# Softmax attention: values in two parts held still in TensorE, weights divided before they are turned, outputs by feature

## The chip, the core and the metric

One core of a Trainium2 chip runs the whole program in one launch. The metric is device time in microseconds (us): 2874.34 us is the median of 3 runs (2862.95 to 2874.93). The engines named below: TensorE (PE; its weight load is PEld), VectorE (DVE), ScalarE (ACT), GpSimd (POOL), and SyncE (SP), which issues nearly all transfers. TensorE writes to PSUM (8 banks of 128 x 512 fp32); the other tiles lie in SBUF, 128 partitions wide.

## The reference

Two small networks run one behind the other on 512 tokens of width 1024: two layers of mixer, cross attention and MLP, then two layers of mixer and mixture of experts. The change bears on the softmax attentions over 512 tokens with 64 features a head:

```python
# forgetting: 8 heads; causal
p = softmax(where(mask, q @ k.T * scale + c_q - c_k, -inf)); out = p @ v
# dilated: 8 heads, three dilation patterns merged; sliding window of 128 with a sink: 8 heads
out = num * w / (den * w + exp(sink - m2))
# nsa: 16 heads in 4 groups; three branches, gated and added
o_cmp = masked_softmax(q @ kc.T + bias) @ vc         # 31 compressed keys
o_sel = masked_softmax(q @ k_sel.T + bias) @ v_sel   # causal
o_win = masked_softmax(q @ k_win.T + bias) @ v_win   # causal
return gt[0] * o_cmp + gt[1] * o_sel + gt[2] * o_win
```

Everything is float32. With 512 tokens the selection and the window of nsa take in every causal key, so these two branches are plain causal attention.

## The kernel before

**Exact products from split operands.** A float32 operand is split into a high part in the type `float32r` and the rest: ScalarE copies (`L107`, for weights `L130`), VectorE subtracts (`L108`, `L131`). A linear layer is three `float32r` products (`mm3`, L151 to L153), whose outputs are copied or added from the two banks of tag `lin`. Weights come in pieces of 128 x 1024 (`piece`, L123): buffers `ws` (4), `wh` and `wl` (3 each).

**Attention.** Queries come in four blocks of 128, keys in blocks of 128 up to the query's; 10 pairs of blocks a causal head, 7 for the sliding window. For each head and query block `probs` (L289) makes scores in a PSUM bank of tag `s` (two products, L296; with negated queries, so that the largest weight has the smallest number), VectorE adds the bias strip and takes the minimum (L301, L302: one instruction and a second that reads the accumulator), and ScalarE writes `P`, the exponential, and its sum `den` (L304). `pv` (L307) then turns `P` block by block on TensorE (L312), copies it to SBUF on ScalarE or VectorE in turn (`copy`, L783 on VectorE), and multiplies: the turned weights are the stationary operand and 64 columns of plain fp32 values move past them (L316). All eight outputs of a pair of heads stand in one PSUM bank by query. Only then are they divided (`o_norm`, L318; for nsa `gated`, L1740, with the gates: L1749, L1751), turned to features (`pair_out`, L326, L332) and split for the output layer.

Pairs of heads follow each other: four in `ab` (forgetting), four dilated and four sliding in `cd`, eight in `nsa`, each with two causal branches for two heads and a compressed branch. The projection of the next pair stands between them in the code.

**What sets the order.** The program is written against a tile framework. A tile has a tag, and a tag has so many buffers (`BUFS`, L17; `BANKS` for PSUM); who needs a buffer waits for its last reader. The framework also puts the instructions of each engine in an order of its own, so that projections and output layers stand between those of attention; on the chip each engine goes through its list in that order.

Of the kernel before, what the change touches and what calls it, by code (L numbers as in the profile page):

```python
# [33 lines left out]
class Kern:  # L34
# [235 lines left out]
    def k_parts(self, y, name="K", tag="x"):  # L270
# [3 lines left out]
        K, L = self.pair(name, tag, F32R), self.pair("KL", tag, F32R)  # L274
# [14 lines left out]
    def probs(self, qk, nk, strip, mn, den, extra=None, floor=None):  # L289
# [14 lines left out]
        nc.scalar.activation(P[:, :nk], p[:, :nk], AF.Exp, bias=mn, scale=-1.0, accum_out=den)  # L304
# [13 lines left out]
    def o_norm(self, o, den, heads):  # L318
        r = self.small((128, heads), "rden")
        self.nc.vector.reciprocal(r, den)  # L320
        ob = self.t("ob")
        v = lambda x: x.rearrange("p (h d) -> p h d", h=heads)
        self.nc.vector.tensor_tensor(v(ob), v(o), r[:, :, None].to_broadcast([128, heads, S // heads]), op=OP.mult)
        return ob

# [38 lines left out]
    def ab(self):  # L364
# [8 lines left out]
        v = self.tiles("v", 4, "x")  # L373
# [5 lines left out]
        def ev_v(c, t, p):  # L379
            nc.scalar.activation(v[t][:, c * 256:(c + 1) * 256], p, AF.Copy, scale=rms()[0][:, t:t + 1])  # L380
# [47 lines left out]
        def attend(i):  # L428
            mn, den = self.small((128, 8), "mn"), self.small((128, 8), "den")
            o = self.psum("pt")  # L430
            for j in range(8):
                qb, e = NT - 1 - j // 2, j % 2
                h, nk, qs = 2 * i + e, (qb + 1) * 128, slice(qb * 128, (qb + 1) * 128)
                u = 8 * qb + h
                P = self.probs(self.qk(*parts[i], e, qs, slice(0, nk)), nk, self.fstrip, mn[:, j:j + 1], den[:, j:j + 1],
                               extra=(at[:, u:u + 1].to_broadcast([128, 128]), crh[:, :nk]))
                self.pv(o[:, j * 64:(j + 1) * 64], P, nk, [v[b][:, h * 64:(h + 1) * 64] for b in range(qb + 1)])
            ys[4 + i] = self.pair("y", "y", F32R)
            self.pair_out(self.o_norm(o, den, 8), ys[4 + i])
# [3 lines left out]
        for i in range(4):  # L443
# [6 lines left out]
            attend(i)  # L450
        ys[:4] = [self.rpair("y") for _ in range(4)]
# [71 lines left out]
    def cd(self):  # L523
        nc, V = self.nc, VCOL
        xs, rms = self.rms_prep(self.hT, V["cd_norm"])
        C, Sn = self.pair("CS")
# [12 lines left out]
        v = self.tiles("v", 4, "x")  # L539
        vd_ = self.t("vd")  # L540
        vd = [vd_[:, t * 128:(t + 1) * 128] for t in range(NT)]

        def ev_v(c, t, p):
            nc.scalar.activation(v[t][:, c * 256:(c + 1) * 256] if c < 2 else vd[t], p, AF.Copy, scale=rms()[0][:, t:t + 1])
# [18 lines left out]
        def dilated(i):  # L563
            mn, den = self.small((128, 8), "mn"), self.small((128, 8), "den")
            o = self.psum("pt")
            for j in range(8):
                qb, e = NT - 1 - j // 2, j % 2
                h, nk, qs = 2 * i + e, (qb + 1) * 128, slice(qb * 128, (qb + 1) * 128)
                P = self.probs(self.qk(qp[i], *kp[i], e, qs, slice(0, nk)), nk, self.dstrip[:, 512 - nk:],
                               mn[:, j:j + 1], den[:, j:j + 1])  # L570
                self.pv(o[:, j * 64:(j + 1) * 64], P, nk, [v[b][:, h * 64:(h + 1) * 64] for b in range(qb + 1)])
            self.pair_out(self.o_norm(o, den, 8), ys[i])

        def sliding(i):

            mn, den = self.small((128, 8), "mn"), self.small((128, 8), "den")
            o = self.psum("pt")
            for j in range(8):
                qb, e = NT - 1 - j // 2, j % 2
                h, k0, qs = i + 4 * e, max(0, qb - 1) * 128, slice(qb * 128, (qb + 1) * 128)  # L580
                nk = (qb + 1) * 128 - k0
                P = self.probs(self.qk(qp[4 + i], *kp[4], e, qs, slice(k0, k0 + nk)), nk, self.sstrip[:, 256 - nk:],
                               mn[:, j:j + 1], den[:, j:j + 1], floor=self.nsink[:, h:h + 1])
                self.pv(o[:, j * 64:(j + 1) * 64], P, nk,
                        [vd[k0 // 128 + b][:, e * 64:e * 64 + 64] for b in range(nk // 128)])
            x = self.small((128, 8), "es")
            sinks = self.nsink.rearrange("p (e i) -> p i e", e=2)[:, i]
            nc.vector.tensor_tensor(x.rearrange("p (t e) -> p t e", e=2), mn.rearrange("p (t e) -> p t e", e=2),
                                    sinks[:, None].to_broadcast([128, NT, 2]), op=OP.subtract)
            nc.scalar.activation(x, x, AF.Exp)  # L590
            nc.vector.tensor_tensor(den, den, x, op=OP.add)
            ys.append(self.rpair("y"))
            self.pair_out(self.o_norm(o, den, 8), ys[4 + i])
# [11 lines left out]
        for i in range(8):  # L605
# [5 lines left out]
            (dilated if i < 4 else sliding)(i % 4)  # L611
        for j in range(8):
# [511 lines left out]
    def out_moe(self, wname, ys, layer, out=None):  # L1124

        nc = self.nc
        z = [self.T("z", "y" if layer == 0 else "h") for _ in range(NT)]
# [94 lines left out]
    def ln_out(self, z, layer, out, yg, w, y, ohT, w15):  # L1222
# [16 lines left out]
        def add(t):  # L1239
# [4 lines left out]
            Rs[t] = self.T("R", "h" if layer == 0 else "y")  # L1244
# [63 lines left out]
    def moe(self, layer, lg, Rs, z, rescale):  # L1308
# [76 lines left out]
        xT, oh = self.dispatch(layer, 0, Rs, pos3, iota, "h" if layer == 0 else "y")  # L1385
# [627 lines left out]
```

## Time and profile before

| What | Value |
|---|---|
| Profiled execution | 2872.59 us, of which 2870.8 us are the span of the core |
| TensorE busy | 2684.3 us (94%), weight loads 2290.8 us (80%) |
| VectorE busy | 1783.8 us (62%) |
| ScalarE busy | 1368.9 us (48%) |
| GpSimd busy | 231.1 us (8%) |
| Granted TensorE clock, mean | 0.972 |

Busy shares are means over stages with different limits; the attention stages are some 476 us of the span. A busy TensorE is not one at its peak, since the records of one matmul overlap the next. The same holds on VectorE and ScalarE: a record begins before the one ahead of it has ended.

### The profile page before, as it was taken

How to read it: one execution, taken by the hardware profiler on the slowest of the kernel's cores; microseconds unless marked ns; L12 is line 12 of the kernel's file. 1: busy time of each engine (PE TensorE's matmuls, PEld its weight loads, DVE VectorE, ACT ScalarE, POOL GpSimd, SP SyncE). 2: the span in 40 equal slices, each digit the busy share in tenths (PEclk: the TensorE clock that was granted, in tenths of full speed). 3: DMA queues.
4: the chain of work that ended last, by engine and by line, in shares of the span. 5: the costliest groups of instructions: out<-in, count | busy, mean ns of one | idle time of the engine just before them, and what ended most of it. 6: DMA issues, size and time to landing. Idle time of an engine off the chain costs nothing. (4 is left out here: it accounts for less than half of the span.)

```text
span 2870.8 us, 40089 instructions
## 1 busy us (share of the span) xinstructions
PE 2684.3 (94%) x15088; PEld 2290.8 (80%) x15088; DVE 1783.8 (62%) x3539; ACT 1368.9 (48%) x2545; POOL 231.1 (8%) x207
## 2 busy tenths in 40 slices
PE   8999999999999999999999999969986999986994
PEld 6888888888888988888887888967865888885873
DVE  6675564444457556545347777677766477677667
ACT  5654442333356434332246444327763355525774
POOL 1101010000111010000010000020001011011001
PEclk9999999999999999999999999979998999997998
DMA  4314133333233322335323222327885202013786
GB/s 134 98 56 137 60 107 96 96 95 99 86 88 85 125 78 63 104 100 176 99 93 120 69 69 80 103 65 244 263 282 181 66 23 74 16 49 128 260 264 218
DMA packets 123112, 333.65 MB, mean 116 GB/s; under 512 B 21781, under 2 KB 37813, under 8 KB 122905
## 3 DMA queue, kind: packets, MB, share of 16 engines
q1 hardware_dynamic: 120472, 322.48, 35.8%
q0 software_dynamic: 2432, 8.46, 0.8%
q8 instruction: 124, 2.03, 0.3%
q14 instruction: 84, 0.68, 0.1%
HBM read 301.49 MB, written 29.07 MB: 115 GB/s over the span
## 5 line engine op out<-in xcount | busy, mean ns | idle before, releaser
L130 ACT ACTIVATE wh<-ws 128x1024 fp32r<-128x1024 f32 (+2 forms) x521 | 534.1, 1030 | 888.5 <-PE lin L152 609.5
L131 DVE TENSOR_TENSOR wl<-ws,wh 128x1024 fp32r<-128x1024 f32 (+2 forms) x521 | 622.1, 1199 | 230.8 <-ACT wh L130 228.7
L151 PE MATMUL lin<-xs,wh 128*128 128x512 f32 (+2 forms) x1080 | 427.3, 396 | 7.7 <-ACT xs L196 6.3
L152 PE MATMUL lin<-xs,wh 128*128 128x512 f32 (+2 forms) x1080 | 427.7, 396 | 2.6 <-DVE xs L197 2.6
L153 PE MATMUL lin<-xs,wl 128*128 128x512 f32 (+2 forms) x1080 | 426.5, 395 | 0.9 <-DVE wl L131 0.9
L151 PEld LDWEIGHTS lin<-xs,wh 128*128 128x128 f32 (+2 forms) x1080 | 202.1, 187 | 51.0 <-ACT xs L196 7.2
L152 PEld LDWEIGHTS lin<-xs,wh 128*128 128x128 f32 (+2 forms) x1080 | 202.2, 187 | 47.2 <-DVE xs L197 6.9
L153 PEld LDWEIGHTS lin<-xs,wl 128*128 128x128 f32 (+2 forms) x1080 | 202.1, 187 | 42.1 <-DVE wl L131 1.4
L346 DVE TENSOR_TENSOR h<-lin,h 128x512 f32<-128x512 f32 x112 | 77.4, 691 | 247.7 <-PE lin L153 247.6
L151 PE MATMUL lin<-sr,wh 128*128 128x512 f32 x512 | 199.2, 389 | 0.0
L152 PE MATMUL lin<-sr,wh 128*128 128x512 f32 x512 | 199.2, 389 | 0.0
L153 PE MATMUL lin<-sr,wl 128*128 128x512 f32 x512 | 199.2, 389 | 0.0
L733 DVE SCALAR_TENSOR_TENSOR ra<-lin,bc 128x512 f32<-128x512 f32 x64 | 44.3, 692 | 166.8 <-PE lin L153 164.3
L1519 PE MATMUL o<-oh,Rh 128*128 128x256 f32 x512 | 133.5, 293 | 8.1 <-PEq L1380 4.9
L304 ACT ACTIVATE P<-s,mn 128x256 f32<-128x256 f32 (+1 forms) x224 | 114.2, 514 | 52.4 <-DVE mn L302 50.0
L1519 PE MATMUL o<-oh,Rl 128*128 128x256 f32 x512 | 132.1, 290 | 3.7 <-PEq L1380 3.7
L152 PE MATMUL s<-wl,exh 128*128 128x512 f32 x256 | 106.2, 415 | 12.7 <-DVE wl L131 12.6
L151 PE MATMUL s<-wh,exh 128*128 128x512 f32 x256 | 102.9, 405 | 12.3 <-ACT wh L130 12.1
L153 PEld LDWEIGHTS lin<-sr,wl 128*128 128x128 f32 x512 | 96.1, 188 | 20.1
L152 PEld LDWEIGHTS lin<-sr,wh 128*128 128x128 f32 x512 | 96.1, 188 | 19.9
L151 PEld LDWEIGHTS lin<-sr,wh 128*128 128x128 f32 x512 | 96.1, 188 | 19.8
L1519 PEld LDWEIGHTS o<-oh,Rh 128*128 128x128 f32 x512 | 101.3, 198 | 12.1 <-DVE oh L1508 7.0
(605 smaller groups left out, 6225.0 us busy)
## 6 DMA issues: line engine op xcount, KB each, us to landing
ws<-in_moe_wgu SPq DMA_DIRECT2D x128, 512.0 KB, 5.3
ws<-in_mlp_wu SPq DMA_DIRECT2D x64, 512.0 KB, 3.6
ws<-in_mlp_wd SPq DMA_DIRECT2D x64, 512.0 KB, 3.6
ws<-in_moe_wd SPq DMA_DIRECT2D x64, 512.0 KB, 5.2
yd<-ey SPq DMA_DIRECT2D x60, 256.0 KB, 3.3
ws<-in_gdn_w SPq DMA_DIRECT2D x24, 512.0 KB, 3.6
ws<-in_ab_w SPq DMA_DIRECT2D x16, 512.0 KB, 4.3
ws<-in_xa_wk SPq DMA_DIRECT2D x16, 512.0 KB, 3.8
```

Of the source, the lines that this page charges most:

```text
L130: nc.scalar.activation(wh, ws, AF.Copy)
L131: nc.vector.tensor_tensor(wl, ws, rd(wh), op=OP.subtract)
L151: mm(out, a[0], b[0], start=start, stop=False)
L152: mm(out, a[0], b[1], start=False, stop=False)
L153: mm(out, a[1], b[0], start=False, stop=stop)
L304: nc.scalar.activation(P[:, :nk], p[:, :nk], AF.Exp, bias=mn, scale=-1.0, accum_out=den)
L346: self.nc.vector.tensor_tensor(self.hT[n], p, self.hT[n], op=OP.add)
L733: nc.vector.scalar_tensor_tensor(a, p, 0.0, rms()[1], op0=OP.max, op1=OP.mult)
L1519: nc.tensor.matmul(p[:, j * 256:(j + 1) * 256], Rs[t][i][:, f * 128:(f + 1) * 128], oh[:, t], start=t + i == 0, stop=t == NT - 1 and i == 1)
```

## The change

The values are split too, and both parts of one head, 64 columns high and 64 low, are now the stationary operand. The turned weights move past them, split in two as well, 128 columns a query block, and two query blocks share one instruction. The output stands by feature, high parts in partitions 0 to 63 and low parts in 64 to 127, and `head_out` adds the halves. Since the query now lies along the free axis, the division by `den` (and the gate) moves ahead of the turn: one reciprocal on VectorE and one multiplication on GpSimd for each `P`. `o_norm`, `gated` and `pair_out` go out of these attentions. The sink enters as one more column of the exponential (a small ScalarE copy).

```diff
+        if sink is not None:
+            n += 1
+            nc.scalar.activation(p[:, nk:n], sink, AF.Copy)
+        nc.scalar.activation(P[:, :n], p[:, :n], AF.Exp, bias=mn, scale=-1.0, accum_out=den)
         return P
 
...
+    def weigh(self, P, nk, den, gate=None):
+
+        r = self.small((128, 1), "rd")
+        self.nc.vector.reciprocal(r, den)
+        if gate is None:
+            self.nc.gpsimd.tensor_scalar(P[:, :nk], P[:, :nk], r, None, op0=OP.mult)
+        else:
+            self.nc.gpsimd.tensor_scalar(P[:, :nk], P[:, :nk], r, gate, op0=OP.mult, op1=OP.mult)
+
+    def turn(self, Ps, PT):
+
+        p, n = self.psum("o"), 0
+        for P, nb in Ps:
+            for b in range(nb):
+                self.nc.tensor.transpose(p[:, n * 128:(n + 1) * 128], P[:, b * 128:(b + 1) * 128], self.ident)
...
+        self.split(p[:, :n * 128], *(x[:, :n * 128] for x in PT))
...
+    def causal(self, o, P, V, first=True, last=True):
+
+
+        mm = self.nc.tensor.matmul
+        PT = self.turned()
+        for qb in (3, 2):
+            self.turn([(P(qb), qb + 1)], [x[:, (qb - 2) * 512:(qb - 1) * 512] for x in PT])
+
+        for k, i in ((0, 0), (1, 0), (1, 1), (3, 0), (3, 1), (2, 0), (2, 1), (0, 1)):
+            x = PT[i].rearrange("p (q c) -> p q c", q=2)[:, k // 3:, k * 128:(k + 1) * 128]
+            mm(o[:, 256 + k // 3 * 128:], V(k), x, start=first and k + i == 0, stop=False)
+        PT = [self.t("PT", F32R, "PT") for _ in range(2)]
+        p1 = P(1)
+        self.turn([(P(0), 1), (p1, 2)], PT)
+        for k, i in ((0, 0), (1, 0), (1, 1), (0, 1)):
+            mm(o[:, k * 128:256], V(k), PT[i][:, k * 256:256 + k * 128], start=False, stop=last and (k, i) == (0, 1))
+
+    def head_out(self, e, o, y):
+
+        u = self.t("oh")[:64]
+        self.nc.scalar.activation(u, o[64:], AF.Copy)
+        self.nc.vector.tensor_tensor(y[e * 64:e * 64 + 64], o[:64], u, op=OP.add)
+
+    def v_parts(self, V, p, h, n, r):
+
+        V = V.rearrange("p (h two d) -> p h two d", two=2, d=64)[:, h:h + n]
+        p = p.rearrange("p (h d) -> p h d", d=64)
+        self.nc.scalar.activation(V[:, :, 0], p, AF.Copy, scale=r)
+        self.nc.vector.scalar_tensor_tensor(V[:, :, 1], p, r, rd(V[:, :, 0]), op0=OP.mult, op1=OP.subtract)
 
```

In `ab` (in `cd` likewise; `sliding` makes two turns of two query blocks each, and eight products):

```diff
         def attend(i):
-            mn, den = self.small((128, 8), "mn"), self.small((128, 8), "den")
-            o = self.psum("pt")
-            for j in range(8):
-                qb, e = NT - 1 - j // 2, j % 2
-                h, nk, qs = 2 * i + e, (qb + 1) * 128, slice(qb * 128, (qb + 1) * 128)
-                u = 8 * qb + h
-                P = self.probs(self.qk(*parts[i], e, qs, slice(0, nk)), nk, self.fstrip, mn[:, j:j + 1], den[:, j:j + 1],
-                               extra=(at[:, u:u + 1].to_broadcast([128, 128]), crh[:, :nk]))
-                self.pv(o[:, j * 64:(j + 1) * 64], P, nk, [v[b][:, h * 64:(h + 1) * 64] for b in range(qb + 1)])
+            y = self.t("ob")
+            for e in range(2):
+                h, o = 2 * i + e, self.psum(("pt", "lin")[e])
+
+                def P(qb):
+                    nk, u = (qb + 1) * 128, 8 * qb + h
+                    mn, den = self.small((128, 1), "mn"), self.small((128, 1), "den")
+                    x = self.probs(self.qk(*parts[i], e, slice(nk - 128, nk), slice(0, nk)), nk, self.fstrip, mn, den,
+                                   extra=(at[:, u:u + 1].to_broadcast([128, 128]), crh[:, :nk]))
+                    self.weigh(x, nk, den)
+                    return x
```

In `nsa` the compressed branch is weighted, split and turned at once, and all three branches add up in one PSUM bank a head:

```diff
+            def P(qb):
+                nk, f = (qb + 1) * 128, h * 3 + br + 1
+                mn, den = self.small((128, 1), "mn"), self.small((128, 1), "den")
+                x = self.probs(self.qk(qp[c], *K[c // 4][br], e, slice(nk - 128, nk), slice(0, nk)), nk,
+                               strips[c][:, e * 256 + max(0, 256 - nk):(e + 1) * 256], mn, den)
+                self.weigh(x, nk, den, gt[:, NT - 1 - qb, f:f + 1])
+                return x
+
...
-            L, r = compressed(c)
-            branch(c, 0, acc)
-            if c < 7:
-                if c == 3:
-                    proj_k(1)
-                proj_q(c + 1)
-            compressed_out(c, L, r, acc)
-            branch(c, 1, acc)
```

The wider values need space: they take the four buffers `h`, where the residual stands, during the attentions of `ab` and `cd`. The residual is read again from DRAM after the last head of `ab` (eight transfers of 256 KB, L518 of the new program), and in `cd` written to DRAM at the start (L597) and read back after the dilated heads (L701). In `nsa` the bias strips are loaded pair by pair, and some tiles of the second mixture of experts change places between `h` and `y`.

The new order of each engine. On VectorE, in the middle of `nsa`, before: `L302` are bias and minimum, `PT<-o` is the copy of turned weights, `rg` the reciprocal for a whole pair of heads.

```order
L302 ISA mn_21488 128x1
L783 COPY PT_21558<-o_21554 128x384
L302 ISA s_21589,mn_21488<-s_21589,strip_18300 128x128
L302 ISA mn_21488 128x1
L783 COPY PT_21585<-o_21582 128x256
L302 ISA s_21600,mn_21488<-s_21600,strip_18301 128x128
L302 ISA mn_21488 128x1
L301 TENSOR_REDUCE mf_21671<-s_21667 128x1
L1719 RECIPROCAL rg_21611<-den_21489 128x8
L302 ISA s_21667,mn_21664<-s_21667,strip_18300,mf_21671 128x256
L302 ISA mn_21664 128x1
```

And the same place of the program now: `rd` is the reciprocal of one `P`, `PTwl` and `PT` the low parts of turned weights.

```order
L302 ISA s_24139,mn_24137<-s_24139,strip_23473,mf_24143 128x256
L302 ISA mn_24137 128x1
L335 RECIPROCAL rd_24147<-den_24138 128x1
L301 TENSOR_REDUCE mf_24163<-s_24159 128x1
L108 TENSOR_TENSOR PT_24102<-o_24125,PT_24101 128x384
L302 ISA s_24159,mn_24157<-s_24159,strip_23473,mf_24163 128x256
L302 ISA mn_24157 128x1
L335 RECIPROCAL rd_24167<-den_24158 128x1
L302 ISA s_24188,mn_24186<-s_24188,strip_23473 128x256
L302 ISA mn_24186 128x1
L108 TENSOR_TENSOR PTwl_24136<-o_24150,PTwh_24135 128x512
L335 RECIPROCAL rd_24194<-den_24187 128x1
```

Each minimum is now followed by a reciprocal which needs the sum of the exponential that this minimum starts; it stands directly behind it, or with one instruction between.

On TensorE, before (`L312` turns, `L316` multiplies turned weights and values, `x2` are two such in a row):

```order
L296 MATMUL s_21589<-KL_21378,Q_21459 128x128
L296 MATMUL s_21600<-K_21377,Q_21459 128x128
L316 MATMUL pt_21490<-vv_20839,PT_21558 128x64 x2
L316 MATMUL pt_21490<-vv_20840,PT_21558 128x64
L316 MATMUL pt_21490<-vv_20839,PT_21572 128x64 x2
L312 MATMUL o_21582<-c_ident,P_21579 128x128 x2
L312 MATMUL o_21595<-c_ident,P_21592 128x128
L296 MATMUL s_21600<-KL_21378,Q_21459 128x128
L296 MATMUL s_21667<-K_21418,Q_21459 128x512
L296 MATMUL s_21667<-KL_21419,Q_21459 128x512
L316 MATMUL pt_21490<-vv_20839,PT_21585 128x64 x2
```

And now (`L346` turns; `L365` and `L370` multiply, with the values still):

```order
L346 MATMUL o_22609<-c_ident,P_22601 128x128 x4
L346 MATMUL o_22629<-c_ident,P_22621 128x128 x3
L296 MATMUL s_22647<-K_21968,Q_22171 128x256
L296 MATMUL s_22647<-KL_21969,Q_22171 128x256
L296 MATMUL s_22658<-K_21968,Q_22171 128x128
L296 MATMUL s_22658<-KL_21969,Q_22171 128x128
L1772 MATMUL s_22678<-kc_21758,Q_22589 128x64
L365 MATMUL pt_22470<-PTwh_22594,vv_21372 128x256
L365 MATMUL pt_22470<-PTwh_22594,vv_21373 128x256
```

The products with values are fewer and wider, and stand in blocks behind the turns of a whole head.

## Rows read from the trace of the kernel before

**Rows 1.** Busy time in three stretches: us, then engines (instructions), PEclk, DMA share, GB/s
```profile
128.40:199.20 70.80, 65.57 (x440) 56.77 (x438) 54.70 (x164) 45.81 (x118) 8.76 (x11) 1.00 0.14 41
819.90:992.00 172.10, 168.09 (x1151) 152.11 (x1151) 122.77 (x282) 106.28 (x252) 19.05 (x17) 0.97 0.34 99
2287.30:2520.80 233.50, 225.06 (x1609) 203.04 (x1607) 168.52 (x565) 130.42 (x369) 25.19 (x45) 0.98 0.12 37
```

**Rows 2.** The middle stretch again, its two attention parts alone
```profile
819.90:940.00 120.10, 116.09 (x732) 100.37 (x731) 91.07 (x233) 80.98 (x210) 19.05 (x17) 0.97 0.28 75
...
982.00:992.00 10.00, 10.00 (x85) 9.74 (x85) 7.31 (x15) 6.10 (x13) 0.00 (x0) 1.00 0.51 169
```

**Rows 3.** Instructions of L316 and L1703: count, ns min/median/max, first and last start
```profile
L316 PE MATMUL pt<-vv,PT x640: 217/275/421, 2291.4 to 2523.7; 128*128 128x64 f32 x160
...
L316 PE MATMUL pt<-v,PT x320: 217/275/323, 132.7 to 895.9; 128*128 128x64 f32 x160
...
L316 PE MATMUL pt<-vd,PT x112: 217/275/421, 899.4 to 994.2; 128*128 128x64 f32 x112
...
L1703 PE MATMUL pt<-BD,PTc x64: 270/275/354, 2301.5 to 2513.6; 128*128 128x128 f32 x64
```

**Rows 4.** Order of time, TensorE: start us, us, engine line op out<-in xcount
```profile
2302.87 0.60 PE L312 MATMUL o<-c_ident,P 128*128 128x128 f32 x4
...
2303.49 0.28 PE L296 MATMUL s<-K,Q 128*128 128x256 f32 x1
...
2303.61 0.28 PE L296 MATMUL s<-KL,Q 128*128 128x256 f32 x1
...
2304.19 1.89 PE L316 MATMUL pt<-vv,PT 128*128 128x64 f32 x16
```

**Rows 5.** VectorE groups by shape, 2287.3 to 2520.8: xcount | busy us, mean ns | idle before
```profile
L1749 DVE SCALAR_TENSOR_TENSOR acc<-pt,rg,acc 128x64 f32<-128x64 f32 x56 | 11.4, 278 | 1.4 <-PE pt L316 1.2 <-POOL ovx L1452 0.2
L783 DVE COPY PT<-o 128x512 f32<-128x512 f32 x16 | 11.0, 688 | 3.9 <-PE o L312 3.8
...
L783 DVE COPY PT<-o 128x384 f32<-128x384 f32 x16 | 8.9, 558 | 15.3 <-PE o L312 15.2
...
L783 DVE COPY PT<-o 128x256 f32<-128x256 f32 x15 | 6.4, 425 | 13.6 <-PE o L312 12.2 <-PE s L296 1.2
...
L1751 DVE TENSOR_TENSOR acc<-pt,rg 128x512 f32<-128x512 f32 x8 | 5.5, 691 | 0.9 <-PE pt L316 0.4
...
L783 DVE COPY PT<-o 128x128 f32<-128x128 f32 x15 | 4.3, 290 | 4.5 <-PE o L312 4.1
L1719 DVE RECIPROCAL rg<-den 128x8 f32<-128x8 f32 x15 | 3.0, 202 | 5.4 <-ACT P L304 5.2
```

**Rows 6.** VectorE groups by shape, whole run: its smallest reciprocal
```profile
L699 DVE RECIPROCAL den<-den 128x2 f32<-128x2 f32 x16 | 2.6, 160 | 1.8 <-ACT P L697 1.8
```

**Rows 7.** Order of time, from a minimum on VectorE to its exponential on ScalarE
```profile
2393.47 0.14 DVE L302 DVE_READ_ACCUMULATOR2_ANT mn<- 128x1 f32 x1
...
2393.88 0.48 DVE L302 CUSTOM_DVE_ANT_0 s<-s,strip,mf 128x256 f32<-128x256 f32 x1
2394.24 0.19 ACT L304 ACTIVATION_READ_ACCUMULATOR P<-s,mn 128x1 f32 x1
2394.28 0.14 DVE L302 DVE_READ_ACCUMULATOR2_ANT mn<- 128x1 f32 x1
...
2394.93 0.19 ACT L304 ACTIVATION_READ_ACCUMULATOR P<-s,mn 128x1 f32 x1
```

**Rows 8.** Lines L206, L197 and L1753: xcount: ns min/median/max, first and last start
```profile
L206 POOL TENSOR_TENSOR ssq<-ssq,sq x48: 725/1770/2268, 11.8 to 1509.7; 128x512 f32<-128x512 f32 x42, 128x256 f32<-128x256 f32 x6
...
L197 DVE SCALAR_TENSOR_TENSOR xs<-h,vec,xs x56: 739/747/1809, 6.2 to 1509.6; 128x512 fp32r<-128x512 f32 x56
...
L1753 POOL TENSOR_TENSOR acc<-acc,gtmp x8: 1268/1277/1286, 2303.5 to 2514.8; 128x512 f32<-128x512 f32 x8
```

**Rows 9.** Transfers by line: count, KB each, median us to landing
```profile
h<-in_xT SPq DMA_DIRECT2D x8, 256.0 KB, 5.2
```

More of the change, by code (lines that the diff above doesn't have):

```diff
@@ L563, in dilated @@
         def dilated(i):
[L564 to L571, printed above, removed]
@@ L572, in dilated @@
-            self.pair_out(self.o_norm(o, den, 8), ys[i])
-        def sliding(i):
[L576 to L591, printed above, removed]
@@ L592, in sliding @@
             ys.append(self.rpair("y"))
-            self.pair_out(self.o_norm(o, den, 8), ys[4 + i])
+            self.split(y, *ys[4 + i])
         def proj(i):
@@ L1126, in out_moe @@
         nc = self.nc
-        z = [self.T("z", "y" if layer == 0 else "h") for _ in range(NT)]
+        z = [self.T("z", "y") for _ in range(NT)]
         for t in range(NT):
@@ L1723, in nsa @@
         proj_k(0)
         proj_q(0)
+        PT = compressed(0)
         for c in range(8):
[L1726 to L1734 removed]
+            y = self.t("ob")
+            for e in range(2):
+                o = self.psum(("pt", "lin")[e])
+                nc.tensor.matmul(o, BD[:, c // 4 * 2 + e], PT, start=True, stop=False)
+                for br in range(2):
+                    branch(c, br, e, o)
+                    if c < 7 and e == 0:
+                        if br:
+                            PTn = compressed(c + 1)
+                        else:
+                            if c == 3:
+                                proj_k(1)
+                            proj_q(c + 1)
+                self.head_out(e, o, y)
+            PT = PTn
@@ L1735, in nsa @@
             if c >= 4:
-                ys.append(self.rpair("ny"))
-            self.pair_out(acc, ys[c])
+                ys.append(self.pair("ny", "h", F32R))
+            self.split(y, *ys[c])
         self.dump_ys("d_ny", ys)
         self.ys = ys
-    def gated(self, acc, o, r, first, last=False):
-        nc = self.nc
-        h8 = lambda x: x.rearrange("p (h d) -> p h d", h=8)
-        d = acc if first else self.t("gtmp")
-        if last:
-            for j in range(8):
-                sl = slice(j * 64, (j + 1) * 64)
-                nc.vector.scalar_tensor_tensor(acc[:, sl], o[:, sl], r[:, j:j + 1], acc[:, sl], op0=OP.mult, op1=OP.add)
-            return
-        nc.vector.tensor_tensor(h8(d), h8(o), r[:, :, None].to_broadcast([128, 8, 64]), op=OP.mult)
-        if not first:
-            nc.gpsimd.tensor_tensor(acc, acc, d, op=OP.add)
```

151 lines of the change are left out of this document (95 added, 56 removed).

## The prediction

> **What bounds the kernel now.** I read the page's engine shares first, then the attention stages alone, since a mean over the span says nothing of them; then the groups by shape, for prices; then the order of time, for what one record costs beside the next; last the new order of instructions. The three stretches in which `probs` runs take 70.8, 172.1 and 233.5 us [rows 1]. TensorE is busy for 93%, 98% and 96% of them, VectorE for 77%, 71% and 72%, ScalarE for 65%, 62% and 56%, at a granted clock of 0.97 to 1.00 of 2.4 GHz. So TensorE sets the pace, and VectorE is next. The middle stretch has 42 us in which cross attention's keys and values run; its attention proper is 130.1 us with VectorE busy for 98.4 [rows 2].
>
> **TensorE.** Sixteen records of the product with values take 1.89 us, the last 0.28 us of which is one record's own length: 0.107 us each [rows 4]. `nsa` has 8 pairs x 2 heads x 2 branches x 10 block pairs = 320 such products, but 640 records; `ab` with the dilated heads has 160 and 320, the sliding heads 56 and 112 [rows 3]. An fp32 product is two records, so it costs 0.214. Four turns take 0.60, so a turn costs 0.107, and a `float32r` product of 256 columns 0.12 [rows 4]. One of 128 columns has no dense row; the 64-column record is its floor (0.107), 256 columns its ceiling; I take 0.12.
> - A causal head: 10 x 0.214 = 2.14 becomes 8 products of 256 columns and 4 of 128, 12 x 0.12 = 1.44. Two turns of `pair_out` go, 0.21. Gain 0.91, for 48 heads (nsa's branches counted singly) 43.7 us.
> - A sliding head: 7 x 0.214 = 1.50 becomes 8 x 0.12 = 0.96, and 0.21: 0.75, x 8 = 6.0.
> - The compressed branch: 64 records, 6.8 us [rows 3, 4], become 16 products of 512 columns (two of 256 each: 3.8) and 16 more turns (1.7): 1.3.
>
> Together 51 us: 7.3 in `ab`, 13.3 in `cd`, 30.4 in `nsa`. If TensorE still set the pace, all of it would show.
>
> **VectorE.** A record begins 0.08 us before the one ahead ends (2393.88 + 0.48 against 2394.28) [rows 7], so an instruction costs its mean less 0.08: 512 columns out of PSUM 0.61, 384 0.48, 256 0.34, 128 0.21 [rows 5]. A reciprocal of one column has no row; the narrowest, of two, costs 0.08 [rows 6], the one of eight 0.12 [rows 5]; nothing speaks for less than the narrowest's half. I take 0.08.
> - A causal head: three subtractions of 512, 384 and 384 columns (1.57) and four reciprocals (0.32) come; half of four copies (0.82) goes, since the copies alternate with ScalarE. Plus 1.07.
> - A pair in `ab` or dilated: 2 x 1.07, two half sums in `head_out` (priced as 512 columns, 1.22), less `o_norm` (0.61 + 0.12): 2.63. Four pairs each: 10.5 and 10.5.
> - A sliding pair: 2 x (0.61 + 0.48) + 0.64 + 1.22, less half of eight copies (1.23), `o_norm` (0.73) and two small ones (0.15): 1.93, x 4 = 7.7.
> - A pair in `nsa`: 4 x 1.07 + 1.22 and 0.47 for the split of the compressed weights, less eight gated sums (11.4/56 = 0.20 each, 1.6), two gated products (1.22) and two reciprocals with gates (0.4) [rows 5]: 2.75, x 8 = 22.0.
>
> Together 50.7 us, as much as TensorE gains.
>
> **The added wait.** Each new reciprocal waits for an exponential that VectorE itself has just started. From the end of the minimum to the end of ScalarE's sum it is 2394.43 - 2393.61 = 0.82 us for 512 columns and 2395.12 - 2394.42 = 0.70 for 384 [rows 7]; VectorE could have gone on 0.08 earlier, so 0.90 and 0.78 (by the same step of 0.12, 0.66 for 256 columns and 0.54 for 128). VectorE takes its list in order, so the subtractions for which TensorE waits are queued behind it. In the new order of `nsa` 50 of 128 reciprocals stand directly behind their minimum: 16 of 512 columns, 24 of 384, 8 of 256, 2 of 128, 39.5 us. For the other 78 I took off the price of what stands between; 13 us stay. `ab` has 6 of 32 directly behind and 8 us in all, `cd` 14 of 64 and 15.3.
>
> VectorE's own line, busy time plus work plus waits:
> - `ab`: 54.7 + 10.5 + 8.0 = 73.2, against 70.8;
> - `cd` without its 42 us: 98.4 + 18.2 + 15.3 = 131.9, against 130.1;
> - `nsa`: 168.5 + 22.0 + 52.9 = 243.4, against 233.5.
>
> Sum +14.1. The busy time counts records to their end, and the waits begin 0.08 before it; about 100 waits are of any length, 8 us counted twice. So +6.
>
> **What else is added.** ScalarE gets a copy for each subtraction and half sum and eight small ones for the sinks; priced as VectorE's, with the same copies gone, 11, 25 and 34 us on 45.8, 106.3 and 130.4 [rows 1]. It is then busy for 70 to 80%, so this hides, and would cost nothing until VectorE's line were shorter. GpSimd gets 224 multiplications of 320 columns on average. No row has its one-input multiplication; a two-input one of 512 columns takes 1.28 [rows 8], 0.8 for 320, the upper end; half is the lower. At the upper end GpSimd is busy for 232 of 476 us, no bound, and the delay to the turn lies beside the next scores. The residual's reload (eight transfers, 5.2 us each [rows 9]) stands on SP's queue behind five pieces of weights and waits for the last product; 132 products of keys and values (15.8 us) follow on TensorE. Hidden; uncovered it would cost two or three transfers' time, 10 to 16 us, as would the reload in `cd`.
>
> Where GpSimd and VectorE both read SBUF there is a price already: GpSimd's sums at L206 have a median of 1.77 us for what L1753 does in 1.28, and VectorE's L197 goes from 0.74 to 1.81 [rows 8]. The new multiplications meet VectorE's weight splits and two-input subtractions, about 140 in the new order of the three stretches; I add 4 us, a fifth of what the second rival below works out.
>
> **Sum.** 2872.6 + 6 + 4 = 2882.6, on the profiled execution (2870.8 span and 1.8 around it), which lies 1.75 below the median of the runs; a gain on TensorE of 51 us turned into a change of bound. I take 2883; this case's own range is 2867 to 2899.
>
> **Rivals.**
> *The gain comes through.* The waits behind minima stand where VectorE would have idled anyway, and other work fills them. Then `ab` goes by VectorE's 65.2, `cd` by 116.6, `nsa` by TensorE's 225 - 30.4 = 195 or VectorE's 190.5; with the 5% that TensorE now leaves open, 68.5 + 122.5 + 205 = 396 against 434.4: -38, so 2835. For it: half of `cd`'s and most of `ab`'s reciprocals have an instruction between. Against it: the 50 in `nsa`.
> *GpSimd and VectorE shut each other out.* Each weight split, query split or output split on VectorE that meets a multiplication waits for its end, and its successors with it. GpSimd would be busy 38% of the stretches with multiplications; a meeting costs half of 0.8 us; 140 x 0.38 x 0.4 = 21 us, and about as much the other way, where the multiplication waits and the turn comes late. Of the latter I count a third, so 28 in place of 4: 2907. It decides once multiplications take 0.8 us rather than 0.4. For it: L197's and L206's longest [rows 8]. Against it: L1753 ran at 1.27 to 1.29 each time, beside VectorE instructions that read PSUM, which most here do.
> The Trainium skill, page "SBUF — State Buffer", section "SBUF: two separate sides", states this as an exclusive lock: a GpSimd instruction and a VectorE instruction with two SBUF inputs exclude each other for the whole instruction. The trace agrees as far as L206 and L197 go; by that rule alone the time is this rival's.
>
> **Chances.** Forecast 0.55, gain 0.27, lock 0.18. The range of 8 in 10 leaves a tenth on each side: low inside the first rival (2831), high in the second (2908). What this kernel's runs can tell from no change is about 0.5%, 14 us, so 2860 and 2889: faster 0.29 (the first rival, and 0.03 of the forecast), same 0.37, slower 0.34 (most of the second, and a third of the forecast).
>
> **What would show it.** In the profile after: TensorE's busy share in the `nsa` stretch falls below 90% and VectorE's idle time before L335 is 50 to 80 us, released by ScalarE's L308; products at L365 start 0.12 apart; GpSimd's L339 has a mean near 0.4 (no lock) or above 0.8 (lock); idle time before the additions of the residual stays as it was. I am wrong if the three stretches shrink together by over 15 us, or if the loss lies outside them.

## The result and the profile after

The changed kernel takes 3077.59 us (median of 4 runs, 3075.24 to 3080.61), the one before beside it 2874.64: a ratio of 1.0709, 95% interval 1.0686 to 1.0732. I had forecast 2883, with 2908 as the upper end. The profiled span is 3073.5 us, 202.7 longer than before. The three attention stretches, from the first bias-and-minimum instruction of a stage to the last, after the change (columns as in [rows 1]):

```profile
126.20:236.90 110.70, 84.20 (x359) 68.17 (x360) 69.95 (x204) 58.55 (x135) 42.42 (x41) 0.73 0.06 20
859.30:1106.10 246.80, 194.46 (x1011) 160.93 (x1009) 146.20 (x346) 129.03 (x301) 89.55 (x80) 0.79 0.25 77
2399.60:2721.80 322.20, 254.37 (x1272) 192.30 (x1272) 198.77 (x644) 164.11 (x426) 100.12 (x170) 0.89 0.09 30
sum 679.70, PE 533.03 PEld 421.40 DVE 414.93 ACT 351.69 POOL 232.09; mean PE 177.68 PEld 140.47 DVE 138.31 ACT 117.23 POOL 77.36
```

Against [rows 1] they grew by 40, 75 and 89 us, 203 together: the whole loss. No engine is full. TensorE waits for 147 us where it waited for 18; its granted clock is 0.73 to 0.89 in the mean of the stretches, so part of its records ran at 1.2 GHz, and its busy time grew from 459 to 533 although it has less to do. VectorE is busy for 61%, ScalarE for 52%, GpSimd for 34%.

One block of weights of a dilated head, 512 columns, in order of time on all engines (start us, us, engine line op; lines left out are marked):

```profile
904.57 0.68 DVE L302 CUSTOM_DVE_ANT_0 s<-s,c_dstrip 128x512 f32<-128x512 f32 x1
...
905.17 0.14 DVE L302 DVE_READ_ACCUMULATOR2_ANT mn<- 128x1 f32 x1
...
905.39 1.59 POOL L606 TENSOR_TENSOR zr<-zr,CS 128x512 f32<-128x512 f32 x1
905.40 0.69 ACT L308 ACTIVATE P<-s,mn 128x512 f32<-128x512 f32 x1 [0.94 <-DVE mn L302]
...
906.21 0.16 DVE L335 RECIPROCAL rd<-den 128x1 f32<-128x1 f32 x1 [0.36 <-ACT P L308]
...
906.96 2.10 POOL L337 TENSOR_SCALAR P<-P,rd 128x512 f32<-128x512 f32 x1
...
909.11 1.12 PE L346 MATMUL o<-c_ident,P 128*128 128x128 f32 x4 [1.46 <-POOL P L337]
...
911.31 0.60 ACT L107 ACTIVATE PTwh<-o 128x512 fp32r<-128x512 f32 x1
...
911.94 0.69 DVE L108 TENSOR_TENSOR PTwl<-o,PTwh 128x512 fp32r<-128x512 f32 x1
...
912.42 0.49 ACT L107 ACTIVATE PTwh<-o 128x384 fp32r<-128x384 f32 x1 [0.51 <-PE o L346]
...
913.03 0.72 PE L365 MATMUL lin<-PTwh,v 128*128 128x256 f32 x2
```

From the end of the minimum (905.31) to the first product it is 7.7 us: 0.9 until the sum is there, 0.8 for the reciprocal and until GpSimd is through with a rotation that stands ahead on its list, 2.1 for the multiplication, 1.1 for the turn, 1.1 until ScalarE comes to the copy, 0.6 for the copy, and then the second block's copy, since a product takes two query blocks. In brackets is what each engine waited for. I call each such step a link of the chain. A block of the same shape in the kernel before:

```profile
882.67 0.14 DVE L302 DVE_READ_ACCUMULATOR2_ANT mn<- 128x1 f32 x1
882.91 0.69 ACT L304 ACTIVATE P<-s,mn 128x512 f32<-128x512 f32 x1
...
884.27 0.60 PE L312 MATMUL o<-c_ident,P 128*128 128x128 f32 x4
...
886.89 1.04 PE L316 MATMUL pt<-v,PT 128*128 128x64 f32 x8
```

There the turn began 1.5 us after the minimum's end and the first product 4.1 us after it; now it is 3.8 and 7.7. Who waited for the exponential, over the whole run (us, times), and TensorE's longest waits (total us, times, longest) in `ab`, in `cd` and, three lines, in `nsa`; last the whole list for `nsa` before:

```profile
  DVE rd L335: 61.4, 85
  PEld s L296: 55.0, 75
  PE s L296: 35.7, 60
```

```profile
PE o L346 <- POOL P L337: 11.1, 12, 3.2
...
PE o L346 <- POOL P L337: 31.5, 26, 3.1
...
PE s L296 <- ACT P L308: 18.4, 46, 2.0
PE o L1792 <- DVE Lp L108: 16.4, 8, 2.7
PE o L346 <- POOL P L339: 13.3, 36, 1.3
```

```profile
PE o L312 <- ACT P L304: 5.3, 3, 3.1
PE pt L316 <- ACT PT L781: 1.3, 7, 0.2
PE pt L316 <- DVE PT L783: 0.4, 2, 0.2
```

Turns wait for GpSimd, 56 us in the three stretches; scores wait for the exponential to free one of three score banks; and the turn of the compressed branch (L1792) waits for its new split. The prices of GpSimd by shape, whole run, and the reciprocal that answers to [rows 6]:

```profile
L337 POOL TENSOR_SCALAR P<-P,rd 128x512 f32<-128x512 f32 x16 | 25.5, 1596 | 32.0 <-DVE rd L335 24.1 <-DVE u L240 4.0 <-PE o L346 3.6
L339 POOL TENSOR_SCALAR P<-P,rd,gt 128x512 f32<-128x512 f32 x32 | 24.6, 768 | 51.8 <-DVE rd L335 47.0 <-DVE mf L301 2.5 <-PE pt L370 2.3
...
L335 DVE RECIPROCAL rd<-den 128x1 f32<-128x1 f32 x224 | 35.6, 159 | 64.5 <-ACT P L308 61.4 <-POOL P L337 0.7
```

L337 (`ab`, `cd`) has one scalar, L339 (`nsa`) two, the gate being the second; with one scalar the same 512 columns take twice as long. (`P<-P,rd` is the multiplication, in place.)

### The profile page after: what moved, and what is told of

The parts are those of the page before. It is cut to its first block, busy times and chain, and to the rows that moved or that the text cites. A ratio compares the mean times of both kernels' runs of the same rounds, so it can differ in the third digit from the quotient of the medians.

```text
span 3073.5 us, 39796 instructions
## 1 busy us (share of the span) xinstructions
PE 2758.3 (90%) x14544; PEld 2301.8 (75%) x14544; DVE 1862.9 (61%) x3739; ACT 1439.4 (47%) x2681; POOL 416.1 (14%) x431
## 5 line engine op out<-in xcount | busy, mean ns | idle before, releaser
L346 PE MATMUL o<-c_ident,P 128*128 128x128 f32 x536 | 114.8, 334 | 59.0 <-POOL P L337 43.2
L308 ACT ACTIVATE P<-s,mn 128x512 f32<-128x512 f32 (+1 forms) x224 | 115.2, 514 | 92.1 <-DVE mn L302 87.1
L346 PEld LDWEIGHTS o<-c_ident,P 128*128 128x128 f32 x536 | 74.3, 167 | 90.6 <-POOL P L337 55.5
L337 POOL TENSOR_SCALAR P<-P,rd 128x256 f32<-128x256 f32 (+2 forms) x96 | 110.5, 1152 | 211.6 <-DVE rd L335 183.0
L296 PE MATMUL s<-K,Q 128*128 128x512 f32 (+1 forms) x224 | 96.2, 432 | 41.0 <-ACT P L308 35.7
L206 POOL TENSOR_TENSOR ssq<-sq,sq 128x512 f32<-128x512 f32 (+1 forms) x8 | 12.2, 1523 | 817.1 <-ACT sq L201 791.7
```

Of the source, the lines that this page charges most:

```text
L296: nc.tensor.matmul(p[:, :nk], q, k, start=i == 0, stop=i == len(qk) - 1)
L308: nc.scalar.activation(P[:, :n], p[:, :n], AF.Exp, bias=mn, scale=-1.0, accum_out=den)
L337: self.nc.gpsimd.tensor_scalar(P[:, :nk], P[:, :nk], r, None, op0=OP.mult)
L346: self.nc.tensor.transpose(p[:, n * 128:(n + 1) * 128], P[:, b * 128:(b + 1) * 128], self.ident)
```

## The experiments

Each kernel but the changed one ran once, beside a run of the kernel before on the same chip; those runs lay between 2865 and 2880. So two times that lie within some 15 us of each other are not told apart here, and the stretches are read beside them. Us; TensorE's columns are its busy and idle time in the three stretches.

| Kernel | Time | Before beside it | ab | cd | nsa | Sum | PE busy | PE idle |
|---|---|---|---|---|---|---|---|---|
| before | 2874.6 | | 71 | 172 | 234 | 476 | 459 | 18 |
| changed | 3077.6 | 2874.6 | 111 | 247 | 322 | 680 | 533 | 147 |
| e1 multiplication on VectorE | 3084.0 | 2879.6 | 103 | 235 | 336 | 673 | 536 | 137 |
| e2 two scalars | 3066.6 | 2879.6 | 102 | 241 | 326 | 669 | 539 | 130 |
| e3 no division | 4439.2 | 2879.6 | 85 | 218 | 274 | 576 | 473 | 104 |
| e4 five P | 3155.1 | 2879.6 | 110 | 249 | 326 | 685 | 539 | 147 |
| e5 extra products | 3080.9 | 2879.2 | 104 | 255 | 327 | 685 | 576 | 109 |
| e7 two heads | 3096.0 | 2879.2 | 114 | 249 | 341 | 703 | 554 | 149 |
| e8 before, divided | 2979.2 | 2879.2 | 103 | 197 | 302 | 602 | 532 | 70 |
| e9 columns | 3049.9 | 2879.2 | 85 | 245 | 301 | 632 | 506 | 125 |
| e6 high part only | 3024.1 | 2873.6 | 95 | 233 | 297 | 624 | 503 | 121 |
| e10 columns, two scalars | 3032.0 | 2873.6 | 80 | 236 | 303 | 619 | 501 | 119 |
| e11 e10, two heads | 3022.2 | 2873.6 | 89 | 217 | 308 | 615 | 495 | 120 |
| e12 e8 with columns | 2932.6 | 2873.6 | 91 | 199 | 251 | 541 | 499 | 42 |
| e14 e10, one bank | 3013.6 | 2875.7 | 80 | 232 | 298 | 609 | 499 | 111 |
| e15 e11, high first | 3030.3 | 2875.7 | 91 | 217 | 312 | 620 | 501 | 119 |
| e16 e11, weights ahead | 3015.7 | 2875.7 | 86 | 218 | 306 | 610 | 498 | 112 |
| e17 e14, no division | 4373.9 | 2865.2 | 78 | 209 | 271 | 558 | 466 | 92 |
| e18 e14, high part only | 2996.6 | 2865.2 | 84 | 224 | 280 | 589 | 484 | 105 |
| e19 e14, neither | 2960.9 | 2865.2 | 78 | 212 | 265 | 555 | 462 | 93 |

**e1**: in `weigh`, `nc.vector.tensor_scalar` for `nc.gpsimd.tensor_scalar`.

> The division and the gate are multiplied in on VectorE instead of GpSimd; all else stays. Theory A, the chain: each block of weights now goes minimum, exponential, reciprocal, multiplication, turn, two-part copy, product, and the engines, which go through their lists in order, wait on it; the GpSimd multiplication (1.15 us in the first two stages, 0.66 in nsa) is its largest new link. VectorE should do it in some 0.3 us, so of the 203 us lost about half comes back: 2960 to 3010, with the idle time before the turns (about 138 us after GpSimd) falling below 70. Theory B, VectorE's own line, which the prediction used: 224 instructions of some 0.3 us more on the engine that sets the pace, so slower than the changed kernel: 3110 to 3150.

3084, the same as the changed kernel within what can be told, against both expectations. VectorE takes 0.54 us where GpSimd took 0.77, and 0.51 in place of 1.60:

```profile
L339 DVE TENSOR_SCALAR P<-P,rd,gt 128x512 f32<-128x512 f32 x32 | 17.2, 538 | 0.0
L337 DVE TENSOR_SCALAR P<-P,rd 128x512 f32<-128x512 f32 x16 | 8.1, 506 | 0.0
```

Its busy time grows by 55 us in the stretches, and no more is lost by that than can be told: VectorE's line is not the bound. Nor is anything gained beyond 7 us of stretches. The sign that the first expectation named did come: TensorE and its weight loads waited 138 us for the multiplication ahead of the turns, and now wait 24 (the changed kernel first, then e1). But in `nsa` the wait for a score bank grew from 18.4 us to 32.1 (last line):

```profile
  POOL P L337: 98.6, 84
  POOL P L339: 39.7, 80
```

```profile
  DVE P L337: 20.2, 28
  DVE P L339: 4.2, 15
```

```profile
PE s L296 <- ACT P L308: 32.1, 47, 1.8
```

The quicker link moved the wait and did not remove it. What GpSimd's multiplications and VectorE could take from each other is gone here too, and the time stays; VectorE's 55 us more could hide a gain, so this alone does not clear the lock.

**e2**:

```diff
-            self.nc.gpsimd.tensor_scalar(P[:, :nk], P[:, :nk], r, None, op0=OP.mult)
+            self.nc.gpsimd.tensor_scalar(P[:, :nk], P[:, :nk], r, self.ones[:, :1], op0=OP.mult, op1=OP.mult)
```

> In the first two stages the GpSimd multiplication gets a second scalar operand of one, as nsa's has its gate; the result is the same. Theory A, the chain, with the form of the instruction at fault for its 1.15 us: the 96 multiplications fall to nsa's lengths (0.48 to 0.77 us by size), 96 x 0.5 = 48 us less in the chain, of which half to all shows: 3030 to 3055. Rival, a lock between GpSimd and VectorE or the neighbours in these stages: the form does not matter, the mean stays near 1.15 us and the time near 3077.

```profile
L337 POOL TENSOR_SCALAR P<-P,rd,ones 128x512 f32<-128x512 f32 x16 | 13.1, 818 | 32.0 <-DVE rd L335 27.2 <-DVE u L240 4.6 <-ACT Q L263 0.3
```

The form is at fault for the length: 1.60 us becomes 0.82. `ab` and `cd` fall by 14 us, the whole by 11, less than expected and less than the time alone can tell.

**e3**: `weigh` returns at once.

> Reciprocal, multiplication and gate are left out in all three stages (the weights are not divided and nsa's branches are not gated), so that only the stationary values, the split turned weights and the output by feature remain of the change. Theory A, the chain through reciprocal and GpSimd: the three stretches fall from 679 us to about 430 to 480, the whole to 2830 to 2880. Rival, the split of the turned weights on two engines one after the other and the order of the heads: most of the loss stays, above 2960.

The stretches fall from 680 to 576: half of the loss, the other half stays. Neither expectation. (The time is not to be compared: 1467 us more lie outside the stretches, where the experts, which get undivided values, run products, `ovx` and `ovw`, that the changed kernel does not run. In e17 they do too.)

**e4**: `"P": 5`, `"ws": 3`.

> Five buffers for the weights P instead of three; for room the raw pieces of weights have three buffers instead of four, which acts on the whole kernel. Theory of buffers: a block of weights is held longer (through reciprocal and multiplication), so its buffers, not the links, hold up the next exponential; with five the stretches shrink by 60 us or more. Theory A, the chain in program order: each engine's list is what waits, and the stretches shrink by less than 25 us.

The stretches do not shrink (685); the 74 us more lie outside them, where raw weights have a buffer less. P's buffers are not it, unless the missing weight buffer cost the stretches as much as they gave.

**e5**:

```diff
         p, n = self.psum("o"), 0
+        for _ in range(2):
+            self.nc.tensor.matmul(p.rearrange("p (a b) -> p a b", a=4), self.identr,
+                                  self.identr[:, None].to_broadcast([128, 4, 128]), start=True, stop=True)
```

> Two products of 512 columns that nobody uses are written into the turn's PSUM bank ahead of each turn (160 turns, 320 products of about 0.22 us at full clock, 70 us of TensorE work). Theory of the clock: in the changed kernel TensorE waits, its granted clock falls to 0.72 to 0.89 in the three stretches, and scores, turns and products, all links of the chain, get up to twice as long; kept busy, the clock stays above 0.95 and the stretches shrink by 30 us or more although work was added: below 3045. Rival: the clock only follows the waits and the added work goes into the chain or beside it: 3077 to 3150.

```profile
126.20:230.00 103.80, 81.37 (x402) 63.93 (x403) 69.63 (x204) 58.30 (x135) 43.29 (x41) 0.89 0.07 21
850.10:1104.60 254.50, 213.93 (x1102) 174.07 (x1101) 149.01 (x349) 132.65 (x303) 87.08 (x80) 0.84 0.26 76
2397.00:2723.80 326.80, 280.95 (x1467) 218.35 (x1467) 199.39 (x644) 166.20 (x427) 100.07 (x170) 0.92 0.10 30
```

The clock rises (0.73 to 0.89 in `ab`), the time does not move, as the rival had it: TensorE's busy time grows by 43 us and its waits shrink by 38. The clock stayed below the 0.95 that the first theory asked for, and what it gave back and what the work took are not separated.

**e7**: the two heads of a pair as generators that yield after each `P` and each turn, taken in turn.

> The two heads of a pair are written in turn, block by block (weights of head 0, weights of head 1, turn of head 0, turn of head 1, and so on), as the kernel before did, instead of one head after the other. Theory of the order: one head at a time leaves one chain in flight, and with two in flight the waits before the turns (138 us after GpSimd) fall by half or more: the stretches from 680 to about 590, the whole 2970 to 3010. Rival, the buffers that both heads share (three score banks, three P, two output banks) let no more than this through: within 15 us of 3077, or slower as the projections lose a bank.

Slower by 18 if anything: two heads in turn do not help by themselves.

**e8**, the division alone, in the kernel before (192 blocks of 224; the sliding heads stay as they were):

```diff
+                d = self.small((128, 1), "den")
-                P = self.probs(..., mn[:, j:j + 1], den[:, j:j + 1])
+                P = self.probs(..., mn[:, j:j + 1], d)
+                self.weigh(P, nk, d)
```

> The kernel before, with one part of the change alone: for the forgetting, dilated and nsa heads each block of weights is divided (and gated) ahead of its turn, reciprocal on VectorE and multiplication on GpSimd; the late division stays in place with a factor of one, so its work is not saved. Values, turns, copies and products by query are as before. If the division in the chain costs by itself what leaving it out gave back (103 us of stretches), the stretches go from 477 to 560 to 590 and the whole to 2960 to 2990. Rival: it hides in the old order with two heads in flight, below 2910, and only together with the split does it cost.

As the first expectation, with stretches 12 us above it: 100 us slower, although values, turns and products are those of before. TensorE idles for 70 us where it idled for 18, and most of that stands where the chain is longer:

```profile
L321 PE MATMUL o<-c_ident,P 128*128 128x128 f32 x536 | 108.8, 305 | 44.8 <-POOL P L312 32.9 <-POOL P L314 7.7 <-ACT P L304 1.2
...
L310 DVE RECIPROCAL rd<-den 128x1 f32<-128x1 f32 x192 | 29.7, 158 | 39.4 <-ACT P L304 38.6
```

**e9**: tiles of one column (floor, minimum, sum, reciprocal) share a tag of eight buffers (`small`, L67), and a block takes three or four of them, the reciprocal's until its multiplication has ended. Now a block has one tile of four columns, with eight buffers (and one-column tiles elsewhere have four). Before, minima and sums stood in tiles of eight columns, one for two heads.

```diff
-            tag, bufs = f"s{n}", 8 if n <= 2 else bufs
+            tag, bufs = f"s{n}", {1: 4, 2: 8, 4: 8}.get(n, bufs)
-                mn, den = self.small((128, 1), "mn"), self.small((128, 1), "den")
+                col = self.small((128, 4), "col")
+                mn, den = col[:, 0:1], col[:, 1:2]
```

> The four narrow numbers of a block (floor, minimum, sum, reciprocal) are columns of one small tile with eight buffers, instead of four tiles that share eight buffers. Theory of the narrow buffers: with three or four of eight taken by each block, a third block's minimum waits for the GpSimd multiplication of the first, in the order of the lists if not in a visible wait; with eight blocks' room the stretches shrink by 40 us or more: below 3040. Rival: these buffers never were the last to come free, within 10 us of 3077.

28 us faster, 48 less in the stretches (20 come back outside them). VectorE's wait at the reciprocal falls from 61.4 to 18.8 us:

```profile
L335 DVE RECIPROCAL col<-col 128x1 f32<-128x1 f32 x224 | 34.9, 158 | 21.8 <-ACT P L308 18.8
```

No long wait in the trace of the changed kernel names these buffers. What changed is the order of the lists: in `nsa` 2 of 128 reciprocals stood behind four or more VectorE instructions since the last minimum, with the columns 24 of 127, so more other work runs while the exponential does.

**e12**: e8 with the same columns.

> The kernel before with the division ahead of the turn (2979, 100 us more than before), now with floor, sum and reciprocal of a block in one small tile with eight buffers. If the narrow buffers are how the division costs, most of the 100 us comes back: below 2920. If the longer chain itself costs, 2955 to 2980.

2933, between the two: 47 us below e8, 41 if each is taken against the run of before beside it, and the wait at the reciprocal falls from 38.6 to 14.6. 59 of the 100 us are left for the longer chain.

```profile
L321 PE MATMUL o<-c_ident,P 128*128 128x128 f32 x536 | 101.7, 299 | 30.1 <-POOL P L312 22.0 <-POOL P L314 4.3 <-ACT P L304 1.2
...
L310 DVE RECIPROCAL col<-col 128x1 f32<-128x1 f32 x192 | 28.0, 157 | 16.2 <-ACT P L304 14.6
```

**e6**: `turn` only copies (ScalarE), and all products read `PT[0]`.

> The changed kernel with the low part of the turned weights left out: ScalarE's copy stays, VectorE's subtraction after it goes, and all products read the high part (as many as before), so the outputs are less exact. Theory of the second link: the two-part copy on two engines one after the other (0.6 + 0.7 us) holds back the products, and with one link the half of the loss that is not the division shrinks: stretches from 680 to below 620, the whole below 3015. Rival: products have slack behind their turn, so only VectorE's work goes and the time falls by less than 25 us.

The stretches fall by 56 us, the time by 53: what was expected but for 4 us in the sum and 9 in the time.

**e10**, **e11**, **e14**: e9 with e2; that with the two heads of e7; e10 with `self.psum("pt")` for both heads' outputs.

> The one tile of small columns together with the second scalar of one in GpSimd's multiplication. If the two gains add up (28 and 11 us) 3039; if the shorter multiplication shows more once a third block may run ahead, 3010 to 3030; if the columns had already hidden the multiplication, 3050.

> As the kernel with columns and two scalars, with the two heads of a pair written in turn, block by block. Theory of the order: two heads in turn cost 19 us alone because the narrow buffers allowed no third block; with eight of them they pay, 40 us or more below the kernel with columns and two scalars. Rival: the order of the engines' lists is made anew in any case and score banks and P let no more through: within 20 us of it.

> Kernel with columns and two scalars, with the outputs of both heads of a pair in the one bank of tag pt, one after the other, so that the projections have both banks of lin again, as in the kernel before. Theory of the bank: head 1's output holds one of the two lin banks through its whole head, and projections and TensorE's filler work wait for the other; with it back 20 us or more below 3032. Rival: the second head's first product now waits for the first head's half sum, and nothing is gained: 3025 to 3060.

e10 is 18 below e9, between the plain sum (3039) and the middle case's upper end; e14 is another 18 below e10, nearly the 20 of its theory; both are hardly more than can be told. e11 is 10 below e10, within what can be told and as the rival had it: two heads in turn do not pay here either.

**e15**, **e16**: e11 with the products' order `(0,0), (1,0), (3,0), (2,0), (1,1), ...`; e11 with `P(3)` and `P(2)` both ahead of their turns.

> Kernel with columns, two scalars and two heads in turn, with all products of the high part of the turned weights written ahead of those of the low part, so that VectorE's subtraction has four products' time more. If the products' wait for the low part is how the subtraction costs its 53 us, 15 us or more below 3022. Rival: it costs as work on VectorE's list, ahead of the next minimum and reciprocal, and the order of the products does nothing: within 8 us of 3022.

> Kernel with columns, two scalars and two heads in turn, with the weights of the query blocks 3 and 2 of a head both written ahead of their turns. If the lists still bring a turn too soon behind its own weights, more weights ahead help: 15 us or more below 3022. Rival: the framework's own order and three P buffers decide, within 10 us of 3022 or slower.

Both within some 8 us of e11, as the rivals had it. In e11 the products' waits for the low part come to 1.6 us over the run (4.6 in the changed kernel), in e15, where the order did change, to none. So the subtraction does not cost through products that wait for the low part.

**e17**, **e18**, **e19**: from e14, without division, without the low part, without either.

> Kernel with columns, two scalars and one output bank (3014, stretches 609 us), with reciprocal, multiplication and gate of the blocks left out; read by its three stretches, since undivided values change the work of the experts behind them. If division and subtraction are two links whose delays add, the stretches fall by about 60 us, what the division cost the kernel before with its columns cleared (541 against 477): 540 to 560. If the chain through both is what counts, by more than 85: below 525.

> The same kernel (stretches 609 us) with the low part's subtraction left out and the products reading the high part. Additive: 56 us less as in the changed kernel, 545 to 565. If most of that was the narrow buffers and the lin bank, which are cleared here, 580 to 600.

> The same kernel with both left out: only the stationary values, their products (as many as in the change), the turn, one copy and the half sums by feature stay of it. If these two links are the whole remaining loss, TensorE's 51 us come through and the stretches are below the 477 us of the kernel before, 425 to 470. If products by feature, in units of two query blocks, cost something of their own, they stay above 490.

Division 51 us (558, as if it were a link by itself), low part 21 (589, so most of e6's 56 were the buffers and the bank), both 55 (555, above 490): the two do not add, and 78 us over the kernel before stay. The stretches of e19:

```profile
126.70:204.30 77.60, 64.51 (x352) 54.78 (x352) 49.66 (x148) 54.34 (x132) 7.66 (x10) 0.91 0.09 28
826.00:1038.00 212.00, 171.44 (x1012) 150.82 (x1010) 116.08 (x245) 125.44 (x301) 17.12 (x17) 0.90 0.30 90
2333.80:2598.90 265.10, 225.92 (x1264) 183.81 (x1263) 128.92 (x420) 157.82 (x421) 19.16 (x43) 0.90 0.11 35
sum 554.70, PE 461.87 PEld 389.42 DVE 294.66 ACT 337.60 POOL 43.94; mean PE 153.96 PEld 129.81 DVE 98.22 ACT 112.53 POOL 14.65
```

TensorE is busy for as long as before (462 against 459), though it does less, at a clock of 0.90; and it waits for 93 us instead of 18: 75 of the 78. In `ab` and `cd` the longest waits are those of a turn for its own exponential (10.3 and 18.9 us, before 4.6 and 1.5), in `nsa` those for a score bank and for the compressed branch:

```profile
PE s L296 <- ACT P L308: 11.3, 16, 1.0
PE o L1790 <- DVE Lp L108: 7.6, 8, 1.3
PE o L341 <- ACT P L308: 5.7, 10, 1.4
```

## Why the prediction was wrong

The step that failed is the sentence on GpSimd: "no bound, and the delay to the turn lies beside the next scores." It does not lie there. The division ahead of the turn alone costs 100 us in the old kernel (e8), where the products and turns are unchanged, and 59 with the narrow buffers cleared (e12); in e8 TensorE waits 41 us for GpSimd ahead of its turns. Reciprocal and multiplication were only tested together: with the multiplication quickened alone the wait moved to the scores (e1). With that sentence fails the method: I added up each engine's own line, busy time plus waits, and took the longest. None of the lines came out: VectorE's line was to be 490 us, `cd`'s 42 us of cross attention included; the stretches take 680 with VectorE busy for 415, and e1 puts 55 us more on that line at no cost that can be told.

- *TensorE's work.* The price was right where products stand close: in `nsa` a quarter of the starts of 256-column products follow within 0.12 us, and 128 columns, priced at 0.12, take 0.06 there; but the medians are 0.17 and 0.11. The sum also took two turns of `pair_out` off each branch of `nsa`, where two branches shared them (`L332`, 32 in the stage): 3.4 of the 51 us were never there. The rest did not show as busy time (459 us before, 462 in e19). My reading, not isolated: the work now comes in pieces (TensorE's records in the stretches join into 51 unbroken ones before, 264 in the changed kernel, 140 in e19), each piece's last record shows its whole length (0.28 us where 256 columns start 0.12 apart [rows 4]), and part of the work runs at the lower clock. By the mean granted clocks, some 109 us of e19's stretches were at 1.2 GHz, against some 20 before.
- *The added wait.* Right in size: 61.4 us at the reciprocals, released by L308, within the 50 to 80 named, and TensorE's share in `nsa` is 79%, below 90. Not seen was that narrow buffers make most of it; with columns it is 18.8 (e9). They cost 41 to 47 us in the old order (e12), 28 in the new.
- *GpSimd's multiplication.* Bounded by 0.4 to 0.8 us: 0.66 in the median of `nsa`, but 1.15 in the mean of the other stages, with one scalar in place of two. Worth 11 to 18 us (e2, e10), single runs at the edge of what can be told.
- *The low part.* Priced at 0.48 to 0.61 us on VectorE's line; leaving it out gives 56 us of stretches in the changed kernel, 21 with the buffers mended, and 3 when the division is gone too (e17 against e19). What a link costs depends on what else is in the chain.
- *The compressed branch.* Priced by its products, turns and split, with no wait; its turn waits 16.4 us for the split in `nsa`.
- *The lin bank.* Not in the prediction; the second head's output holds it, perhaps 18 us (e14).
- *The residual's reload.* Hidden, as said: the additions wait for 246 us over the run, 248 before.
- *Gain comes through.* It did not. Even e19 is slower than before.
- *The lock.* The direction was this rival's, the mechanism was not: without the new multiplications on GpSimd the time is the same (e1). What a lock could lengthen shows in the records of `cd`: VectorE's `L607`, both of whose inputs lie in SBUF, takes 0.85 us beside the multiplications and 0.69 without them (e1), 2 us in eleven; the subtractions, with one input in PSUM, keep 0.69:

```profile
L607 DVE TENSOR_TENSOR z<-z,CS 128x512 f32<-128x512 f32 x11 | 9.4, 854 | 15.7 <-DMA zr<-z 15.7
...
L607 DVE TENSOR_TENSOR z<-z,CS 128x512 f32<-128x512 f32 x11 | 7.5, 685 | 15.5 <-DMA zr<-z 15.5
```

The Trainium skill, "SBUF — State Buffer", section "SBUF: two separate sides", has a GpSimd instruction and a VectorE instruction with two SBUF inputs exclude each other; the trace agrees with that in direction, and what shows of it in VectorE's records here is these 2 us, not 200.

Left open: 78 us that remain in e19. What of the change is in it is known (stationary values, units of two query blocks, copies on ScalarE alone, one head after the other, half sums, the compressed branch by features), not which of these it is; 24 of the 75 us that TensorE waits longer stand before turns that wait for their exponential (35 us against 11). No version here beats the kernel before; the best that holds the values still and leaves nothing out, e14, is 138 us slower.

## What to carry to other kernels

A step put between producer and consumer is not priced by the busy time of its engine: add up one block's way through all engines, with what stands ahead of it on each list, and ask how many blocks may be under way. A quicker link may only move the wait to the next one. Count every buffer that the block holds meanwhile, the narrowest too; here the lists were ordered around them, and no long wait named them. An engine at 95% that gets less work may keep its time, if the work then comes in pieces.

## What the runs showed of the hardware

GpSimd's multiplication of 512 columns took 1.60 us with one scalar and 0.82 with a second scalar of one (e2). VectorE's two-input instruction from SBUF (`L607`) took 0.85 us in the mean beside these multiplications and 0.69 without them (e1). TensorE's granted clock fell from 1.00 to 0.73 in `ab` as its idle time there grew from 5 to 27 us, and rose to 0.89 when products without use were put into the waits, with the same time for the whole (e5).
